# HGRN log decays in a hybrid decoder: one masked product over stacked upper and lower parts of 64 tokens, in place of two over 128

## Chip, cores and metric

The kernel runs on one core of one Trainium2 chip. The metric is the device time of one execution in microseconds. A profiled execution has in addition a span, from the first to the last instruction of the program that the profiler recorded.

## What is computed

The reference is a decoder trunk of two residual layers on 256 tokens of width 1024. Each layer has a token mixer (a group of forgetting-attention heads, "FoX", and a group of eight HGRN2 heads, merged by gates) and a channel mixer (dense SwiGLU in layer 0, eight experts with top-2 routing in layer 1). All is float32. The part that matters here is the HGRN recurrence, chunk by chunk:

```python
HG_CHUNK = 64
...
def hgrn2_recurrence(q, k, v, log_f):
    """S_t = diag(f_t) S_{t-1} + k_t v_t^T, o_t = S_t^T q_t; chunkwise. q,k,log_f: (B,S,H,dk); v: (B,S,H,dv)."""
...
    def step(state, inp):
        q_c, k_c, v_c, g_c = inp
        G = jnp.cumsum(g_c, axis=2)
        diff = G[:, :, :, None, :] - G[:, :, None, :, :]
        decay = jnp.where(causal, jnp.exp(jnp.where(causal, diff, 0.0)), 0.0)
        A = jnp.einsum('bhtk,bhsk,bhtsk->bhts', q_c, k_c, decay)
        o = jnp.einsum('bhts,bhsv->bhtv', A, v_c) + jnp.einsum('bhtk,bhkv->bhtv', q_c * jnp.exp(G), state)
```

So a pair of tokens s < t is weighted, in each of 128 key channels, by the exponential of the sum of the log decays between them.

## The kernel before

The kernel carries no state from chunk to chunk. It treats the 256 tokens as two tiles of 128 (index `i`) and writes every pair of tokens of a tile as one of seven levels (`LV` = 64, 32, ... 1): at level m, a pair lies in two neighbouring runs of m tokens. The decay from s to t is then the product of two exponentials, one from s to the border of the runs and one from the border to t. A further set, the cross decays, leads from the first tile to the second.

All the sums of log decays that these exponentials need are made by TensorE as products with masks of zeros and ones, in `hgrn` (L734). The log decays of a tile, `sg`, are split in `hgrn_in` (L699) into an upper part `lfh` in fp32r (helper `split`, L321, a cast on ScalarE) and the rest `lfl` (a subtraction on VectorE), because a product in fp32r takes its operands rounded. For each tile and head there are two PSUM banks of four masks by 128 tokens, and for each bank two products of 512 columns: L754 with `lfh`, L755 with `lfl`, summed in the bank. The contraction is over the 128 tokens of the tile. ScalarE then takes the exponential of the bank into the tile `e` (name `ee`, L756):

```python
dp = t_bank()
mf = mm.rearrange("p a t -> p (a t)")
pe.matmul(out=dp, lhsT=lfh[:, i, c0:c0 + P], rhs=mf, start=True, stop=False)
pe.matmul(out=dp, lhsT=lfl[:, i, c0:c0 + P], rhs=mf, start=False, stop=True)
a.activation(out=e[:, 4 * mi:4 * mi + 4, h, :], in_=dp.rearrange("p (a t) -> p a t", a=4), func=AF.Exp)
```

VectorE multiplies keys and queries into `e` (L766, L769; L773 to L775 for the last level), TensorE makes the small products of the levels (L785, L787, L798), VectorE gathers them in `aT` (L791 to L804), and TensorE applies them to the values (L808 to L817). There are two layers, two groups of four heads, two pairs of heads in a group and two tiles: sixteen blocks of this kind, each with two heads.

The masks are made once by GpSimd in `build_masks` (L158), during the first projections. `hgrn` is a generator: it yields between its steps, and the projection products around it (L113 to L115 from `mm3`, L411 to L413 from `turned`) advance it by `tick`, so that its steps lie between theirs. In this part of the program a scheduler settles the final order of every engine's instructions when the program is built; each engine then works its own queue in order. Weights of the projections are loaded as `raw`, cast by ScalarE (L93, `whi`) and completed by VectorE (L97, `wlo`). All PSUM tiles named `tb` share four banks, so a new log-decay product can start only when an earlier bank was read.

Of the kernel before, what the change touches and what calls it, by code (L numbers as in the profile page):

```python
# [10 lines left out]
F32 = mybir.dt.float32  # L11
F32R = mybir.dt.float32r
I32 = mybir.dt.int32
AF = mybir.ActivationFunctionType
# [3 lines left out]
P = 128  # L18
# [3 lines left out]
NT = S // P  # L22
# [18 lines left out]
def hybrid_trunk_kernel(  # L41
# [7 lines left out]
    v, a, pe, g = nc.vector, nc.scalar, nc.tensor, nc.gpsimd  # L49
# [4 lines left out]
    pre = pre_stack.enter_context(tc.tile_pool(name="pre", bufs=1, reuse_waits="tile"))  # L54
# [93 lines left out]
    ones = const.tile([P, P], F32, name="ones")  # L148
    g.memset(ones, 1.0)
    ups, iota = (const.tile([P, P], F32, name=n) for n in ("ups", "iota"))  # L150
    mAB = pre.tile([P, 9, P], F32R, tag="masks1", bufs=1, name="mAB")
    mA, mB = mAB[:, :4], mAB[:, 4:]
    mm = pre.tile([P, D], F32, tag="masks2", bufs=1, name="mm")
    cmask, up, tmask = mm[:, 0:256], mm[:, 256:384], mm[:, 384:512].bitcast(I32)
    lmask = mm[:, 512:768].bitcast(I32).rearrange("p (a t) -> p a t", a=4)
# [2 lines left out]
    def build_masks(pool):  # L158
# [7 lines left out]
        mt = u4(pool, "mt", "p (a t) -> p a t", a=8)  # L166
        g.memset(mt, 1.0)
        for li, m in enumerate(LV):
            nb = P // (2 * m)
            w = mt[:, li, :].rearrange("p (b h r) -> p b h r", b=nb, h=2)  # L170
            rt, lf = w[:, :, 1, :], w[:, :, 0, :]
            g.affine_select(out=rt, in_=rt, pattern=[[-2 * m, nb], [0, m]], compare_op=OP.is_ge, fill=0.0, base=-m, channel_multiplier=1)
            g.affine_select(out=rt, in_=rt, pattern=[[2 * m, nb], [1, m]], compare_op=OP.is_ge, fill=0.0, base=m, channel_multiplier=-1)
            g.affine_select(out=lf, in_=lf, pattern=[[-2 * m, nb], [-1, m]], compare_op=OP.is_gt, fill=0.0, base=0, channel_multiplier=1)
            g.affine_select(out=lf, in_=lf, pattern=[[2 * m, nb], [0, m]], compare_op=OP.is_gt, fill=0.0, base=m, channel_multiplier=-1)
        g.affine_select(out=mt[:, 7, :], in_=mt[:, 7, :], pattern=[[-1, P]], compare_op=OP.is_gt, fill=0.0, base=0, channel_multiplier=1)
        g.tensor_copy(mA, mt[:, 0:4])
        g.tensor_copy(mB[:, 0], mt[:, 7])
        g.tensor_copy(mB[:, 1:4], mt[:, 4:7])
        g.tensor_copy(mB[:, 4], up)  # L180
        mk = u4(pool, "mk", "p (a t) -> p a t", n=256, a=4)
        g.memset(mk, 1.0)
        for li, m in enumerate(LV[2:6]):
# [137 lines left out]
    def split(src, hi, lo):  # L321
        a.copy(hi, src)
        v.tensor_sub(lo, src, hi.bitcast(F32))
# [317 lines left out]
    def mixer(l, hT=None, first=None, half_first=None):  # L641
        with tc.tile_pool(name=f"mix{l}", bufs=1, reuse_waits="tile") as mp:
# [20 lines left out]
            if l > 0:  # L663
# [14 lines left out]
                for half in range(2):  # L678
                    tp = t_bank()
# [17 lines left out]
                return hv  # L697

            def hgrn_in(gi):  # L699
                lfh = mp.tile([P, NT, 512], F32R, tag="lfh", bufs=2, name="lfh")  # L700
                lfl = mp.tile([P, NT, 512], F32R, tag="lfl", bufs=2, name="lfl")
                kq = mp.tile([P, 2, NT, 4, P], F32, tag="kq", bufs=2, name="kq")
                c0 = O_HQ + 512 * gi
                for j, bk in enumerate(first.pop(c0) if c0 in first else proj_t(hT, win, c0, 512)):
# [2 lines left out]
                sg, kt = [], []  # L707
# [10 lines left out]
                for i in range(NT):  # L718
                    a.activation(out=sg[i], in_=sg[i], func=AF.Ln)
                for i in range(NT):  # L720
                    split(sg[i], lfh[:, i, :], lfl[:, i, :])
                for i in range(NT):
                    _, tv = transpose4(lambda b: kt[i][:, b * P:(b + 1) * P])
                    dst = kq[:, 0, i]
# [2 lines left out]
                            v.tensor_scalar(out=dst[:, b], in0=tv[:, b], scalar1=omT[:, 4 * gi + b:4 * gi + b + 1], scalar2=None, op0=OP.mult)  # L727
                    else:
                        a.copy(dst, tv)
                return lfh, lfl, kq  # L730

            aTs = []

            def hgrn(gi, lfh, lfl, kq, hv):  # L734
                if not aTs:
                    for _ in range(4):
                        aTs.append(mp.tile([P, 2, P], F32, tag="aT", bufs=4, name="aT"))
# [2 lines left out]
                for hp in range(2):  # L740
# [3 lines left out]
                    ee = []  # L744
                    for i in range(NT):
                        e = mp.tile([P, 8, 2, P], F32, tag="ee", bufs=2, name="ee")
                        ee.append(e)

                        for h in range(2):
                            c0 = (2 * hp + h) * P  # L750
                            for mi, mm in enumerate((mA, mB[:, i:i + 4])):
                                dp = t_bank()
                                mf = mm.rearrange("p a t -> p (a t)")
                                pe.matmul(out=dp, lhsT=lfh[:, i, c0:c0 + P], rhs=mf, start=True, stop=False)  # L754
                                pe.matmul(out=dp, lhsT=lfl[:, i, c0:c0 + P], rhs=mf, start=False, stop=True)  # L755
                                a.activation(out=e[:, 4 * mi:4 * mi + 4, h, :], in_=dp.rearrange("p (a t) -> p a t", a=4), func=AF.Exp)  # L756
                            yield
                        base = kq[:, 0, i, hs, :]
                        lv = [li if li < 4 or i else li + 1 for li in range(7)]
                        cross = 7 if i else 4  # L760
                        for li, m in enumerate(LV[:6]):

                            ev = e[:, lv[li]].rearrange("p h (b s r) -> p (h b) s r", s=2, r=m)
# [14 lines left out]
                        tp = t_bank()  # L778
# [14 lines left out]
                        tp = t_bank()  # L793
                        tv = tp.rearrange("p (a h r) -> p a h r", a=4, h=2)
                        for li, m in enumerate(LV[2:6]):
                            for h in range(2):
                                el = e[:, lv[2 + li], h]
                                pe.matmul(out=tv[:P - m, li, h, :].rearrange("p (b r) -> p b r", r=m), lhsT=el[:, :P - m],  # L798
                                          rhs=el.rearrange("p (b s r) -> p b s r", s=2, r=m)[:, :, 1, :], start=True, stop=True)
# [5 lines left out]
                        yield  # L805
                    tp = t_bank()
                    for h in range(2):
                        pe.matmul(out=tp[:, h * P:(h + 1) * P], lhsT=ee[0][:, 4, h], rhs=ee[1][:, 7, h], start=True, stop=True)  # L808
                    a.copy(aX, tp[:, :2 * P].rearrange("p (h t) -> p h t", h=2))
                    tp = t_bank()  # L810
                    for i in range(NT):
# [994 lines left out]
```

## Time and profile before

| | |
|---|---|
| three runs | 1912.79, 1914.8 and 1915.34 us, median 1914.8 |
| profiled execution, its own time | 1916.2 us |
| its span | 1914.5 us |
| mean granted clock of TensorE | 0.993 of 2.4 GHz |
| instructions | 25527 |
| span, forty slices | TensorE at 90% or more in all but the first two and the last |
| mixers | layer 0 up to about 400 us of the span, layer 1 from about 590 to about 900 |

Times below are counted from the start of the span. PE is TensorE with its products, PEld its weight loads, DVE VectorE, ACT ScalarE, POOL GpSimd. A product's row shows its whole passage, from first operand to last result; the next one can start while it is under way, so that the distance between two starts is shorter than the time shown for one.

### The profile page before, as it was taken

Reading aid. Unit: us, or ns where it says so; the run is one execution under the profiler, and the core shown is the slowest. Engines: PE = TensorE matmul, PEld = TensorE weight load, DVE = VectorE, ACT = ScalarE, POOL = GpSimd, SP = SyncE. Lnnn points to the kernel's source line nnn. Section 1 sums busy time; section 2 is a strip of 40 time slices with the busy share of each in tenths; the row PEclk is TensorE's granted clock in tenths of the full one; section 3 lists DMA queues with packets and bytes.
Section 4 is the critical chain, followed back from the end, with each engine's and each line's share of the span. In section 5 each row is a group of like instructions: output and inputs, shape, how many; then the busy total and the mean of one; then the engine's idle time right before and its main releaser. Section 6 shows DMA issues by size and latency. Waiting matters only on the chain.

```text
span 1914.5 us, 25527 instructions
## 1 busy us (share of the span) xinstructions
PE 1845.4 (96%) x9510; PEld 1534.2 (80%) x9510; DVE 1569.5 (82%) x2006; ACT 1309.9 (68%) x1666; POOL 210.2 (11%) x184
## 2 busy tenths in 40 slices
PE   2999999999999999999999999999999999999998
PEld 2787788889978877788787888888888888888887
DVE  6878865878858887457898989999899989999997
ACT  2467568554436765595788787787887878878775
POOL 6701200000000012100001210003100021000000
PEclk9899999999999999999999999999999999999999
DMA  9543654888855425339899999999999999999990
GB/s 301 167 156 132 220 176 142 299 302 293 314 211 172 140 88 176 120 114 338 293 347 354 349 339 370 362 376 344 340 374 359 375 346 344 368 362 369 358 364 24
DMA packets 235140, 525.50 MB, mean 274 GB/s; under 512 B 11756, under 2 KB 23292, under 8 KB 235008
## 3 DMA queue, kind: packets, MB, share of 16 engines
q1 hardware_dynamic: 233624, 523.61, 76.3%
q8 instruction: 76, 1.25, 0.3%
q14 instruction: 56, 0.46, 0.1%
q10 hardware_dynamic: 1384, 0.18, 0.1%
HBM read 522.72 MB, written 1.05 MB: 274 GB/s over the span
## 4 chain that ended last, share of the span: by engine, by line
PE 74%; DVE 2%; ACT 2%; issue 1%; POOL 1%; DVEq 0%; ACTq 0%; POOLq 0%
PE acc L114 15%; PE acc L115 15%; PE acc L113 15%; PE yb L114 5%; PE yb L115 5%; PE yb L113 5%; PE acc L412 2%; PE acc L413 2%; PE acc L411 2%; PE tb L308 2%; DVE wlo L97 1%; PE tb L1560 1%; PE tb L798 1%; POOL rs L302 1%; PE tb L1290 1%
## 5 line engine op out<-in xcount | busy, mean ns | idle before, releaser
L97 DVE TENSOR_TENSOR wlo<-raw,whi 128x1024 fp32r<-128x1024 f32 (+1 forms) x888 | 1077.1, 1237 | 141.7 <-ACT whi L93 124.5
L93 ACT CAST whi<-raw 128x1024 fp32r<-128x1024 f32 (+1 forms) x888 | 919.3, 1047 | 315.3 <-PE acc L115 183.9
L113 PE MATMUL acc<-whi,g 128*128 128x512 f32 x880 | 349.2, 397 | 0.0
L115 PE MATMUL acc<-whi,g 128*128 128x512 f32 x880 | 344.2, 391 | 0.0
L114 PE MATMUL acc<-wlo,g 128*128 128x512 f32 x880 | 344.1, 391 | 0.0
L113 PE MATMUL acc<-whi,hTh 128*128 128x512 f32 x512 | 210.2, 414 | 4.1 <-ACT hTh L615 4.1
L114 PE MATMUL acc<-wlo,hTh 128*128 128x512 f32 x512 | 206.9, 405 | 5.2 <-DVE wlo L97 5.0
L115 PE MATMUL acc<-whi,hTl 128*128 128x512 f32 x512 | 206.6, 405 | 3.5 <-DVE hTl L617 3.5
L114 PEld LDWEIGHTS acc<-wlo,g 128*128 128x128 f32 x880 | 165.5, 188 | 35.9 <-DVE wlo L97 2.8
L115 PEld LDWEIGHTS acc<-whi,g 128*128 128x128 f32 x880 | 165.1, 188 | 35.7
L113 PEld LDWEIGHTS acc<-whi,g 128*128 128x128 f32 x880 | 165.4, 188 | 32.7
L114 PE MATMUL yb<-wlo,th 128*128 128x512 f32 x440 | 172.5, 392 | 4.1 <-DVE wlo L97 4.1
L115 PE MATMUL yb<-whi,tlo 128*128 128x512 f32 x440 | 171.6, 390 | 0.0
L113 PE MATMUL yb<-whi,th 128*128 128x512 f32 x440 | 171.6, 390 | 0.0
L114 PEld LDWEIGHTS acc<-wlo,hTh 128*128 128x128 f32 x512 | 98.2, 192 | 25.4 <-DVE wlo L97 7.5
L115 PEld LDWEIGHTS acc<-whi,hTl 128*128 128x128 f32 x512 | 97.6, 191 | 24.4 <-DVE hTl L617 5.3
L411 PE MATMUL acc<-hTh,whi 128*128 128x256 f32 x416 | 117.1, 282 | 0.0
L302 POOL TENSOR_TENSOR rs<-rs,mhalf 128x8 f32<-128x8 f32 (+1 forms) x28 | 48.1, 1719 | 623.9 <-DVE rs L301 614.9
L413 PE MATMUL acc<-hTh,wlo 128*128 128x256 f32 x416 | 116.5, 281 | 0.0
L412 PE MATMUL acc<-hTl,whi 128*128 128x256 f32 x416 | 116.3, 280 | 0.0
L113 PEld LDWEIGHTS acc<-whi,hTh 128*128 128x128 f32 x512 | 97.4, 191 | 22.4 <-ACT hTh L615 5.0
L114 PEld LDWEIGHTS yb<-wlo,th 128*128 128x128 f32 x440 | 82.6, 188 | 26.0 <-DVE wlo L97 9.3
(381 smaller groups left out, 2634.8 us busy)
## 6 DMA issues: line engine op xcount, KB each, us to landing
raw<-in_moe_w_gate SPq DMA_DIRECT2D x112, 1024.0 KB, 6.3
raw<-in_moe_w_up SPq DMA_DIRECT2D x112, 1024.0 KB, 5.9
raw<-in_moe_w_down SPq DMA_DIRECT2D x110, 1024.0 KB, 5.6
raw<-in_w_in SPq DMA_DIRECT2D x66, 1024.0 KB, 5.2
raw<-in_w_ada SPq DMA_DIRECT2D x48, 1024.0 KB, 6.8
raw<-in_dense_w_gate SPq DMA_DIRECT2D x10, 1024.0 KB, 8.1
raw<-in_dense_w_up SPq DMA_DIRECT2D x10, 1024.0 KB, 7.8
raw<-in_dense_w_down SPq DMA_DIRECT2D x10, 1024.0 KB, 8.8
```

Source lines behind the costliest of these rows:

```text
L93: a.copy(hi, raw)
L97: v.tensor_sub(lo, raw, hi.bitcast(F32))
L113: pe.matmul(out=o, lhsT=lh, rhs=rh, start=start, stop=False)
L114: pe.matmul(out=o, lhsT=lh, rhs=rl, start=False, stop=False)
L115: pe.matmul(out=o, lhsT=ll, rhs=rh, start=False, stop=stop)
L302: g.tensor_tensor(out=r, in0=r, in1=mhalf[:, :shape[1]], op=OP.pow)
L308: pe.transpose(out=tp[:, b * P:(b + 1) * P], in_=src(b), identity=ident)
L411: pe.matmul(out=o, lhsT=hi, rhs=hT.hh[:, k], start=(k == 0 and c % 2 == 0), stop=False)
L412: pe.matmul(out=o, lhsT=hi, rhs=hT.hl[:, k], start=False, stop=False)
L413: pe.matmul(out=o, lhsT=lo, rhs=hT.hh[:, k], start=False, stop=(k == KD - 1 and c % 2 == 1))
L798: pe.matmul(out=tv[:P - m, li, h, :].rearrange("p (b r) -> p b r", r=m), lhsT=el[:, :P - m], rhs=el.rearrange("p (b s r) -> p b s r", s=2, ...
L1290: pe.matmul(out=tp[:, b * 2 * P:(b * 2 + ne) * P], lhsT=src[:, i, kk * P:(kk + 1) * P], rhs=pair[0]["oneh"][:, i].rearrange("p n t -> p (n ...
```

## The change

`lfh` and `lfl` become two tiles `lf[i]`, one for each token tile, with two halves `b` of 64 tokens. In half b the upper parts of its own 64 tokens lie on these tokens' partitions, and their lower parts on the other 64 partitions. One product with a mask that stands twice, once over each 64 partitions, sums both parts. A bank now holds eight masks by 64 tokens of one half. Only the cross decays need the other half's log decays; for them one product of 64 columns with a column of ones is added to one of the two banks. The mask of the level m = 64 is the one within a half, and is taken from masks that are there already.

```diff
-    mAB = pre.tile([P, 9, P], F32R, tag="masks1", bufs=1, name="mAB")
-    mA, mB = mAB[:, :4], mAB[:, 4:]
+    mAB = pre.tile([P, 2, 9, 64], F32R, tag="masks1", bufs=1, name="mAB")
...
         for li, m in enumerate(LV):
+            if not li:
+                continue
...
-        g.tensor_copy(mA, mt[:, 0:4])
-        g.tensor_copy(mB[:, 0], mt[:, 7])
-        g.tensor_copy(mB[:, 1:4], mt[:, 4:7])
-        g.tensor_copy(mB[:, 4], up)
+
+        for r in (slice(0, 64), slice(64, P)):
+            g.tensor_copy(mAB[r, 0, 2:8], mt[r, 1:7, r])
+            g.tensor_copy(mAB[r, 0, 0:2], mt[r, None, 7, r].to_broadcast([64, 2, 64]))
+            g.tensor_copy(mAB[r, 0, 8], up[r, r])
+        g.tensor_copy(mAB[:, 1], mAB[:, 0])
+        g.tensor_copy(mAB[:, 1, 1], mAB[:, 0, 8])
...
-                lfh = mp.tile([P, NT, 512], F32R, tag="lfh", bufs=2, name="lfh")
-                lfl = mp.tile([P, NT, 512], F32R, tag="lfl", bufs=2, name="lfl")
+
+                lf = [mp.tile([P, 2, 512], F32R, tag=t, bufs=2, name="lf") for t in ("lfh", "lfl")]
...
                 for i in range(NT):
-                    split(sg[i], lfh[:, i, :], lfl[:, i, :])
+                    for b, (own, other) in enumerate(((slice(0, 64), slice(64, P)), (slice(64, P), slice(0, 64)))):
+                        a.copy(lf[i][own, b], sg[i][own])
+                        v.tensor_sub(lf[i][other, b], sg[i][own], lf[i][own, b].bitcast(F32))
...
-                            for mi, mm in enumerate((mA, mB[:, i:i + 4])):
+                            for b in range(2):
                                 dp = t_bank()
-                                mf = mm.rearrange("p a t -> p (a t)")
-                                pe.matmul(out=dp, lhsT=lfh[:, i, c0:c0 + P], rhs=mf, start=True, stop=False)
-                                pe.matmul(out=dp, lhsT=lfl[:, i, c0:c0 + P], rhs=mf, start=False, stop=True)
-                                a.activation(out=e[:, 4 * mi:4 * mi + 4, h, :], in_=dp.rearrange("p (a t) -> p a t", a=4), func=AF.Exp)
+                                whole = b == i
+                                pe.matmul(out=dp, lhsT=lf[i][:, b, c0:c0 + P], rhs=mAB[:, b, i:i + 8].rearrange("p a t -> p (a t)"), start=True, stop=not whole)
+                                if whole:
+                                    pe.matmul(out=dp[:, 7 * 64 * i:7 * 64 * i + 64], lhsT=lf[i][:, 1 - b, c0:c0 + P], rhs=mAB[:, 0, 8, 63:64].to_broadcast([P, 64]), start=False, stop=True)
+                                a.activation(out=e[:, :, h, 64 * b:64 * (b + 1)], in_=dp.rearrange("p (a t) -> p a t", a=8), func=AF.Exp)
...
-                        lv = [li if li < 4 or i else li + 1 for li in range(7)]
-                        cross = 7 if i else 4
+                        lv = [li + 1 - i for li in range(7)]
+                        cross = 7 * i
...
-                        pe.matmul(out=tp[:, h * P:(h + 1) * P], lhsT=ee[0][:, 4, h], rhs=ee[1][:, 7, h], start=True, stop=True)
+                        pe.matmul(out=tp[:, h * P:(h + 1) * P], lhsT=ee[0][:, 0, h], rhs=ee[1][:, 7, h], start=True, stop=True)
```

The scheduler's order moves with this. TensorE in layer 0, at the first log-decay products, before (L411 to L413 are projection products, `tb<-mAB` are the log decays):

```order
L412 MATMUL acc<-hTl,whi 128x256
L754 MATMUL tb<-mAB,lfh 128x512 x2
L413 MATMUL acc<-hTh,wlo 128x256
L411 MATMUL acc<-hTh,whi 128x256
L755 MATMUL tb<-mAB,lfl 128x512 x2
L754 MATMUL tb<-mAB,lfh 128x512
L755 MATMUL tb<-mAB,lfl 128x512
```

And of the change, where the same lines have the numbers L415 to L417, and the log decays L760 (512 columns) and L762 (64 columns):

```order
L416 MATMUL acc<-hTl,whi 128x256
L760 MATMUL tb<-mAB,lf 128x512
L417 MATMUL acc<-hTh,wlo 128x256
L415 MATMUL acc<-hTh,whi 128x256
L416 MATMUL acc<-hTl,whi 128x256
L762 MATMUL tb<-mAB,lf 128x64
L760 MATMUL tb<-mAB,lf 128x512
```

The first log-decay product stands six projection products later than before, and three more stand between it and its bank's second product. In the whole program the order has 128 products of 512 columns on the masks before, and 64 of 512 and 32 of 64 columns in the change; casts to `lfh` and subtractions to `lfl` go from 8 and 8 on 128 partitions to 16 and 16 on 64; table loads of ScalarE go from 57 to 59.

ScalarE in layer 1, where Exp (L756) meets the Silu of the next group's queries (L705), before:

```order
L756 ACTIVATE ee<-tb 128x4x128 x2
L705 ACT_TABLE_LOAD
L705 ACTIVATE kq<-acc 128x2x256
L93 CAST whi<-raw 128x1024 x2
L705 ACTIVATE kq<-acc 128x2x256
L809 COPY aX<-tb 128x256
L756 ACT_TABLE_LOAD
L756 ACTIVATE ee<-tb 128x4x128 x4
```

And of the change (Exp is L763, Silu L709):

```order
L763 ACTIVATE ee<-tb 128x8x64
L709 ACT_TABLE_LOAD
L709 ACTIVATE kq<-acc 128x2x256
L763 ACT_TABLE_LOAD
L763 ACTIVATE ee<-tb 128x8x64
L709 ACT_TABLE_LOAD
L709 ACTIVATE kq<-acc 128x2x256
L93 CAST whi<-raw 128x1024 x2
L816 COPY aX<-tb 128x256
L763 ACT_TABLE_LOAD
L763 ACTIVATE ee<-tb 128x8x64
```

One Exp now stands between the two Silus, and the table is loaded for each of them.

## Rows read from the trace of the kernel before

**Rows 1.** Busy times on the page: us, share of the span, instructions.

```profile
PE 1845.4 (96%) x9510; PEld 1534.2 (80%) x9510; DVE 1569.5 (82%) x2006; ACT 1309.9 (68%) x1666; POOL 210.2 (11%) x184
```

**Rows 2.** Table of stretches, HGRN parts: us by engine, PEclk, DMA share, GB/s.

```profile
100.00:140.00 40.00, 39.81 (x297) 34.97 (x296) 30.42 (x69) 28.88 (x42) 0.00 (x0) 1.00 0.40 128
140.00:200.00 60.00, 58.76 (x372) 48.46 (x373) 48.36 (x119) 38.43 (x57) 7.64 (x4) 1.00 0.38 128
620.00:660.00 40.00, 39.65 (x262) 34.02 (x262) 33.47 (x65) 27.57 (x38) 0.00 (x0) 1.00 0.55 189
660.00:720.00 60.00, 56.97 (x365) 47.66 (x364) 47.10 (x119) 39.36 (x57) 5.96 (x3) 0.97 0.23 73
```

**Rows 3.** Chain of waits, 620 to 740 us: shares by line.

```profile
by line: PE acc L115 12.2%; PE acc L114 12.0%; PE acc L113 11.1%; PE tb L798 11.0%; PE tb L754 5.3%; PE tb L755 4.8%; PE tb L785 4.3%; ACT L756 3.2%; PE acc L412 3.0%; ACT ee L756 2.7%; PE acc L411 2.6%; PE acc L413 2.6%; PE tb L817 2.2%; P
```

**Rows 4.** Timeline of TensorE, layer 0: start us, us, line, operands.

```profile
133.42 0.39 PE L754 MATMUL tb<-mAB,lfh 128*128 128x512 f32 x1
...
134.11 0.39 PE L755 MATMUL tb<-mAB,lfl 128*128 128x512 f32 x1
```

**Rows 5.** Masks' tile: ns min/median/max, first and last start; idle before.

```profile
L754 PE MATMUL tb<-mAB,lfh x64: 387/396/628, 104.4 to 719.7; 128*128 128x512 f32 x64
...
L755 PE MATMUL tb<-mAB,lfl x64: 387/393/628, 105.1 to 719.9; 128*128 128x512 f32 x64
...
L180 POOL CAST mAB<-mm x1: 293/293/293, 78.4 to 78.4; 128x128 fp32r<-128x128 f32 x1
...
  ACT ee L756: 5.3, 5
```

**Rows 6.** Chain of waits, 655 to 672 us: start, us, line, count.

```profile
662.29 1.83 PE tb L798 x16
```

**Rows 7.** Timeline of TensorE: products of 256 columns, six steps.

```profile
120.71 0.28 PE L411 MATMUL acc<-hTh,whi 128*128 128x256 f32 x1
...
121.42 0.28 PE L411 MATMUL acc<-hTh,whi 128*128 128x256 f32 x1
```

**Rows 8.** Tile of the upper parts: its cast and subtraction.

```profile
L322 ACT CAST lfh<-sg x8: 606/616/622, 103.5 to 686.9; 128x512 fp32r<-128x512 f32 x8
L323 DVE TENSOR_TENSOR lfl<-sg,lfh x8: 674/687/693, 104.1 to 687.5; 128x512 fp32r<-128x512 f32 x8
```

**Rows 9.** Groups of ScalarE: busy us, mean ns, idle before.

```profile
L908 ACT ACTIVATE aqk<-tb,prm 66x512 f32<-66x512 f32 x32 | 20.2, 680 | 5.3 <-PE tb L907 5.2
```

**Rows 10.** Timeline of ScalarE, layer 1, an Exp's table load.

```profile
704.85 1.28 ACT L756 ACT_TABLE_LOAD   x1
706.15 0.60 ACT L756 ACTIVATE ee<-tb 128x512 f32<-128x512 f32 x1
```

**Rows 11.** Timeline of TensorE there; idle time in brackets.

```profile
706.80 0.54 PE L754 MATMUL tb<-mAB,lfh 128*128 128x512 f32 x1 [1.79 <-ACT ee L756]
707.14 0.63 PE L755 MATMUL tb<-mAB,lfl 128*128 128x512 f32 x1
...
710.54 0.40 PE L754 MATMUL tb<-mAB,lfh 128*128 128x512 f32 x1
```

**Rows 12.** Table of stretches, 706 to 712 us.

```profile
706.00:712.00 6.00, 5.20 (x16) 4.14 (x17) 3.99 (x11) 3.35 (x6) 2.54 (x1) 0.72 0.43 133
```

**Rows 13.** Tile of the exponentials: durations; who waited for it.

```profile
L766 DVE TENSOR_TENSOR ee<-ee,kq x96: 407/417/460, 108.5 to 724.7; 128x256 f32<-128x256 f32 x96
L756 ACT ACTIVATE ee<-tb x64: 587/598/616, 106.9 to 720.9; 128x512 f32<-128x512 f32 x64
...
L773 DVE TENSOR_TENSOR kq<-kq,ee x16: 280/284/325, 110.9 to 726.4; 128x128 f32<-128x128 f32 x16
L774 DVE RECIPROCAL ee<-ee x16: 933/944/948, 112.2 to 727.3; 128x128 f32<-128x128 f32 x16
...
  PEld tb L785: 5.2, 8
...
  PE tb L785: 2.8, 4
```

More of the change, by code (lines that the diff above doesn't have):

```diff
@@ L729, in hgrn_in, with hgrn @@
                         a.copy(dst, tv)
-                return lfh, lfl, kq
+                return lf, kq
             aTs = []
-            def hgrn(gi, lfh, lfl, kq, hv):
+            def hgrn(gi, lf, kq, hv):
                 if not aTs:
```

## The prediction

> **What bounds the kernel now.** I began with the busy times of the whole span: TensorE's matmuls are busy for 96% of it, VectorE for 82%, ScalarE for 68% [rows 1]. Such a share is an average over stages, so the next view is the table of stretches. The change touches only the HGRN blocks of the two mixers, whose first log-decay product starts at 104.4 us and whose last at 719.7 [rows 5]. In the four stretches that hold nearly all of them TensorE is busy 98.6 of 100 us (layer 0) and 96.6 of 100 (layer 1), VectorE 78.8 and 80.6, ScalarE 67.3 and 66.9, and the DMA queues are far from full [rows 2]. A busy TensorE can still be a stretched one, since its instructions overlap. So the third view is the chain of waits, from 620 to 740 us: 5.3% and 4.8% of these 120 us, 12.1 us together, are the products of L754 and L755, the very ones that the change replaces, and the other large shares are matmuls too [rows 3]. The fourth is the timeline of TensorE: products of 512 columns start every 0.23 us (0.69 us over three steps), although each is shown as 0.39 us long [rows 4]. The price of a product is this step, not its length. The program is thus bound by TensorE's issue in both stretches, with an ordered queue full of projection products that stand between the steps of the HGRN chain.
>
> **The change part by part**, on the profiled execution (1916.2 us, of which 1914.5 are the span; the three runs have a median of 1914.8, so it lies 1.4 us above them).
>
> *Products removed.* L754 and L755 issue 64 products each [rows 5]; the order of the changed kernel has 64 of 512 columns in their place. 64 fewer, at 0.23 us: **-14.7 us**.
>
> *Products added.* 32 of 64 columns, one for each pair of a head and a token tile. No row shows fp32r operands with so few columns. From above: 64-column products of plain f32 take 1.83 us for sixteen, 0.114 each [rows 6], and fp32r products of 256 columns take 0.118 (0.71 us over six steps) [rows 7]. From below: in proportion to columns, 64/512 of 0.23, an estimate of 0.029. I take 0.114, from the row with the same number of columns: **+3.6 us** (+0.9 to +3.8). The Trainium skill has a rule here ("TensorE: Matmul & The Clock Gate", section "Back-to-back issue gap"): products of 1 to 64 columns can start about 25 ns apart. By it the 32 would cost 0.8 us. The f32 row contradicts the rule for its own type, and nothing here shows it for fp32r.
>
> *The split.* Each of the 8 casts to lfh (0.616 us) and 8 subtractions to lfl (0.687 us) becomes two on half the partitions [rows 8]. A ScalarE instruction on 66 partitions and 512 elements takes 0.680 us, no less than one on 128 [rows 9], so half the partitions save nothing: ScalarE gets 8 x 0.616 = 4.9 us more, VectorE 8 x 0.687 = 5.5 us more, each spread over four places. VectorE has 19 to 21 us free in 100, ScalarE 33 [rows 2]. On the path: a complete first bank now needs both halves, so one more subtraction stands ahead of its second product, four times 0.69 = 2.8 us if nothing covers it. The order of TensorE in layer 0 shows six more 256-column products ahead of the first L754, 6 x 0.118 = 0.7 us of cover. I charge **0** (0 to 2.8). Behind the added subtractions on VectorE stand the HGRN multiplications, which wait for the Exp anyway.
>
> *Tables.* The order of ScalarE has 59 table loads instead of 57, the two more in layer 1, where Exp and Silu or Sigmoid now alternate. One load takes 1.28 us: it begins at 704.85, and the Exp behind it at 706.15 [rows 10]. What such a load costs when it meets TensorE is seen in the same place: TensorE waits 1.79 us for that Exp, and the products from 707.14 on take 3.40 us over eight steps, 0.43 each and not 0.23 [rows 11], while the granted clock of the stretch is 0.72, a part of it at 1.2 GHz and not 2.4 [rows 12]. The eight steps lose 1.6 us, so the event costs 3.4. Two new ones would cost 6.8 us, none costs nothing. I take one with a chance of a half: **+1.8 us** (0 to 6.8). The Trainium skill prices a table switch higher ("ScalarE: Activation LUTs", section "What ACT_TABLE_LOAD costs"): 1283 ns and a drain of about 1380, 2.66 us. The row agrees with the first figure alone, as the Exp starts 1.30 us after the load does, 0.02 us behind its end. By the page the two would hold ScalarE 5.3 us, by the row 2.6.
>
> *Exp and its layout.* There are 64 before and after, of 512 elements, 0.598 us each [rows 13]. They now write runs of 64 elements, not 128. I charge 0; what a slower one would do is a rival below.
>
> *Masks.* On POOL four selections go and eight copies stand where four stood. The last mask copy begins at 78.4, the first product that reads it at 104.4 [rows 5]. 25 us cover a few microseconds; without that cover the first HGRN block would wait for them.
>
> Sum: -14.7 + 3.6 + 0 + 1.8 = **-9.3 us**, 1906.9 on the profiled execution, less 1.4: **1905.5 us** as a median. Nothing behind a mixer should give this back, since dense layer and experts start when its last product is done.
>
> **The rivals.**
>
> *A. The narrow products are nearly free.* At the proportional 0.029 us the sum is -14.7 + 0.9 + 1.8 = -12.0, so **1902.8**. For it: 64 columns are an eighth of the work. Against it: both neighbouring rows take 0.11 or more a product [rows 6, 7]. The Trainium skill's rule on few columns, above, would come out within 0.1 us of this. Chance 0.22.
>
> *B. VectorE's chain sets the pace.* A block (16 of them: layers, groups, head pairs, token tiles) gains 11.1/16 = 0.69 us on TensorE, but its chain behind the Exp is untouched: seven multiplications of 0.417, two of 0.284 and a reciprocal of 0.944 us, 4.4 us [rows 13]. VectorE goes to about 81.5 and 83.3 us of a stretch now some 94 long, 0.87 to 0.89. For it: TensorE already waits 5.2 and 2.8 us for these multiplications at L785 [rows 13]. Against it: those are eight of some 190 us, and the order still has projection products to put between. If it holds in half the blocks, half of the 11.1 us goes: -5.6, and with 0.9 for the tables **1910.1**. Chance 0.18.
>
> *C. New waits eat it.* All four subtractions uncovered (2.8) and both table loads as dear as the one at 704.85 (6.8): -14.7 + 3.6 + 9.6 = -1.5, so **1913.3**. For it: the one event seen today shows that a wait is paid twice, by itself and by the clock. Against it: it is seen once today, as three of the four stretches have the full clock and the fourth 0.97 [rows 2]. Chance 0.12.
>
> *D. Slower: the Exp pays for its short runs.* Place: the 64 Exps of L756, which every HGRN block waits for. Nothing in the trace shows an activation that writes runs of 64 with a stride. If each took t longer and none of it were covered, the time would change by 64 t - 9.3, so it decides from 0.15 us on, an Exp of 0.74 us. At twice today's length (t = 0.598) half covered, it is 19.1 - 9.3 = +9.8, so **1924.6**. For it: ScalarE is in the middle of the chain, and TensorE waits for its banks at L754, 5.3 us today [rows 5]. Against it: casts and activations with runs of 512 or 128 elements all take about 0.6. Chance 0.08.
>
> That the change doesn't do what it says is excluded by the order: 128 wide products before, 64 wide and 32 narrow after.
>
> **How the numbers follow.** My forecast gets 0.40, A 0.22, B 0.18, C 0.12, D 0.08. A measurement here can tell about 0.2%, 3.8 us. Forecast and A are faster by more, and most of B (0.15 of its 0.18): faster 0.77. C and the rest of B: the same, 0.15. D: slower, 0.08. The range leaves out C and D, 0.20 in all, on the upper side: 1912.5. Below it takes in A with the event at 704.85 gone as well, -12.0 - 1.8 - 3.4 = -17.2, shortened to -15.8 as both together are unlikely: 1899.0.
>
> **What would show it right or wrong.** Right: 64 wide products 0.23 us apart and 32 narrow ones 0.11 behind which the next starts; the two HGRN stretches each some 4 to 6 us shorter; dense layer and experts as long as before; the chain's share of these products halved. The step at a narrow product decides between the forecast and A. For B, TensorE would wait longer at L785 for VectorE, with VectorE near 0.9 busy. For C, half-speed stretches would stand behind an Exp's table load, or TensorE would wait for lf. For D, the Exp's mean would be over 0.74 us. The forecast is wrong if the two stretches shorten and the end doesn't, for then something behind the mixers, which I take to follow, sets the time.

## The result, and the profile after

The changed kernel is slower. Four runs have a median of 1926.0 us (1922.83 to 1926.77) beside 1913.8 for the kernel before: a ratio of 1.0063, with a 95% interval of 1.0045 to 1.0080, so about 12 us more. The range of the prediction, 1899.0 to 1912.5, does not hold it, and the direction is wrong.

The page after, busy times (answering to [rows 1]), and the table of stretches (to [rows 2]):

```profile
PE 1843.5 (96%) x9478; PEld 1531.6 (80%) x9478; DVE 1574.7 (82%) x2014; ACT 1317.9 (69%) x1676; POOL 211.8 (11%) x184
```

```profile
100.00:140.00 40.00, 37.75 (x261) 33.19 (x260) 29.18 (x63) 28.24 (x41) 0.00 (x0) 0.91 0.37 121
140.00:200.00 60.00, 53.89 (x354) 43.76 (x353) 47.68 (x120) 38.78 (x57) 5.87 (x3) 1.00 0.30 102
620.00:660.00 40.00, 38.72 (x262) 33.24 (x262) 33.98 (x57) 30.37 (x40) 0.00 (x0) 1.00 0.62 213
660.00:720.00 60.00, 55.91 (x354) 45.92 (x355) 49.52 (x126) 43.40 (x62) 5.79 (x3) 0.94 0.22 71
```

TensorE was busy for 195.2 of these 200 us before and is for 186.3 now, its first stretch at a mean clock of 0.91 instead of 1.00 and its last at 0.94 instead of 0.97. The HGRN parts did not get shorter: TensorE has less to do in them and waits more. From the first Ln of a layer to the first FoX product it is 112.0 us before and 119.3 after in layer 0, 114.8 and 115.0 in layer 1. Everything behind a mixer is as long as it was. The profiled execution after is the fastest of the four runs, so the two traces are only 6.6 us apart in span (1914.5 and 1921.1).

The views of the tiles `lf` and `ee` (answering to [rows 5, 8, 13]; L760 are the wide log-decay products of 512 columns, L762 the narrow ones of 64, L726 and L727 the split, L763 the Exp):

```profile
L760 PE MATMUL tb<-mAB,lf x64: 388/477/793, 104.1 to 725.6; 128*128 128x512 f32 x64
...
L762 PE MATMUL tb<-mAB,lf x32: 190/192/403, 104.7 to 725.9; 128*128 128x64 f32 x32
L726 ACT CAST lf<-sg x16: 602/617/622, 102.5 to 687.6; 64x512 fp32r<-64x512 f32 x16
L727 DVE TENSOR_TENSOR lf<-sg,lf x16: 684/686/690, 103.1 to 690.1; 64x512 fp32r<-64x512 f32 x16
its engine sat idle before it (us, times) until:
  ACT ee L763: 11.3, 14
```

```profile
L763 ACT ACTIVATE ee<-tb x64: 587/597/619, 107.4 to 727.0; 128x512 f32<-128x512 f32 x64
```

The Exp takes 0.597 us as before, so rival D's mechanism is not there. Casts and subtractions of 64 partitions cost as much as those of 128, as forecast. What has grown is the waiting: TensorE stands before L760 until an Exp is done for 11.3 us in 14 places, where it was 5.3 us in 5.

The opening of the first head group shows where; a layer has two such openings, each from the Ln of a head group to the first products that need its Exps. ScalarE's timeline before, and after:

```profile
101.13 1.28 ACT L719 ACT_TABLE_LOAD   x1
...
103.48 1.12 ACT L322 CAST lfh<-sg 128x512 fp32r<-128x512 f32 x2
...
106.89 2.06 ACT L756 ACTIVATE ee<-tb 128x512 f32<-128x512 f32 x4
```

```profile
100.15 1.28 ACT L723 ACT_TABLE_LOAD   x1
101.44 1.15 ACT L723 ACTIVATE sg<-sg 128x512 f32<-128x512 f32 x2
102.50 2.53 ACT L726 CAST lf<-sg 64x512 fp32r<-64x512 f32 x4
105.06 1.07 ACT L735 COPY kq<-tb 128x512 f32<-128x512 f32 x2
106.15 1.28 ACT L763 ACT_TABLE_LOAD   x1
107.44 2.06 ACT L763 ACTIVATE ee<-tb 128x512 f32<-128x512 f32 x4
109.53 2.94 ACT L93 CAST whi<-raw 128x1024 fp32r<-128x1024 f32 x3
```

ScalarE works here without a gap, in a fixed order: Ln, casts, copies, table load, Exp, and then the casts of the next projection weights. The Exp begins 5.76 us after the Ln's table load before and 7.29 after; 1.41 of the 1.53 us are the two more casts. TensorE's timeline and the clock behind it, after:

```profile
108.18 0.28 PE L417 MATMUL acc<-hTh,wlo 128*128 128x256 f32 x1
110.63 0.38 PE L415 MATMUL acc<-hTh,whi 128*128 128x256 f32 x1 [2.17 <-DVE ee L773]
```

```profile
112.80:119.60 6.80, 6.80 (x30) 6.32 (x29) 2.62 (x7) 3.66 (x5) 0.00 (x0) 0.50 0.15 28
```

TensorE runs out of projection products, waits 2.17 us for the first multiplication behind the Exps (L773), and then has 6.8 us at half the clock, 1.2 GHz, in which it does 3.4 us less than at full. Before, it waited 0.2 us at the same place. That suggested the first theory: **theory 1**, the split costs it, through ScalarE's order. Against it stood **theory 2**, the products cost it, and later a third, that the scheduler's new order does.

### The profile page after: what moved, and what is told of

It is laid out like the page before. It is cut to its first block, busy times and chain, and to the rows that moved or that the text cites. A ratio compares the mean times of both kernels' runs of the same rounds, so it can differ in the third digit from the quotient of the medians.

```text
span 1921.1 us, 25483 instructions
## 1 busy us (share of the span) xinstructions
PE 1843.5 (96%) x9478; PEld 1531.6 (80%) x9478; DVE 1574.7 (82%) x2014; ACT 1317.9 (69%) x1676; POOL 211.8 (11%) x184
## 4 chain that ended last, share of the span: by engine, by line
PE 74%; DVE 2%; ACT 2%; POOL 1%; issue 0%; DVEq 0%; ACTq 0%; POOLq 0%
PE acc L114 15%; PE acc L115 15%; PE acc L113 15%; PE yb L114 5%; PE yb L115 5%; PE yb L113 5%; PE acc L415 2%; PE acc L417 2%; PE acc L416 2%; PE tb L312 2%; DVE wlo L97 1%; PE tb L1567 1%; POOL rs L306 1%; PE tb L805 1%; PE tb L1297 1%
## 5 line engine op out<-in xcount | busy, mean ns | idle before, releaser
L415 PE MATMUL acc<-hTh,whi 128*128 128x256 f32 x416 | 117.6, 283 | 2.2 <-DVE ee L773 2.2
L417 PE MATMUL acc<-hTh,wlo 128*128 128x256 f32 x416 | 116.9, 282 | 0.4 <-DVE wlo L97 0.4
```

What stands on the lines that cost most here:

```text
L415: pe.matmul(out=o, lhsT=hi, rhs=hT.hh[:, k], start=(k == 0 and c % 2 == 0), stop=False)
L417: pe.matmul(out=o, lhsT=lo, rhs=hT.hh[:, k], start=False, stop=(k == KD - 1 and c % 2 == 1))
```

## Experiments

**Parts alone, each with the order that the scheduler makes for it.**

```diff
# e1_split_alone (in the kernel before)
-                    split(sg[i], lfh[:, i, :], lfl[:, i, :])
+                    for r in (slice(0, 64), slice(64, P)):
+                        split(sg[i][r], lfh[r, i, :], lfl[r, i, :])
# e2_products_alone (in the changed kernel, in place of its casts and subtractions)
+                    split(sg[i], lf[i][:, 0], lf[i][:, 1])
# e3_pool_casts (in the changed kernel)
-                        a.copy(lf[i][own, b], sg[i][own])
+                        (g.tensor_copy if b else a.copy)(lf[i][own, b], sg[i][own])
# e5_no_narrow (in the changed kernel): L762 left out
```

> The kernel before with one part of the change: the split is done in halves of 64 partitions (4 casts and 4 subtractions for a head group instead of 2 and 2, each written to its old place), the products are the old ones. Theory 1 (the split costs it: the added casts stand in ScalarE's order ahead of the first Exp and of the next weights' casts, TensorE runs dry, then its clock falls): slower than before by 4 to 12 us, 1918 to 1926, with a wait of TensorE over 1 us and a stretch at half clock in layer 0 near 110 us. Theory 2 (the products cost it: the wide product behind a narrow one, the banks and the cover that TensorE's saved work gave): within 3 us of before, 1911 to 1917, no new half-clock stretch.

> The changed kernel with the old price of the split: two casts and two subtractions of 128 partitions for a head group, written to the two new tiles, so that the products read other rows than they should (the log decays of both parts are mixed, the values are not the reference's; the products, their shapes and their order stay). Theory 1: faster than before by 6 to 11 us, 1903 to 1908. Theory 2: slower than before by over 3 us still, 1917 or more.

> The changed kernel with the casts of the lower 64 tokens on POOL, which has nothing else to do there: ScalarE is back to two casts for a head group, VectorE keeps its four subtractions. Theory 1, if POOL's copies take no more than 1.6 us each: at least 6 us faster than the changed kernel, 1908 to 1920, and the first Exp of layer 0 about 1.2 us earlier behind the Ln. Theory 2: 1922 to 1929, as the changed kernel.

> The changed kernel without its 32 narrow products (left out, so that the whole-prefix level lacks the other half's sum). Theory 1: they and the dearer step of the wide product behind them cost 32 x 0.115 = 3.7 us, so 1920 to 1924. Theory 2: with them goes the dear step and the wait for banks behind it, 1904 to 1914.

Measured, as ratios to before: the split alone 1.0008 (0.9999 to 1.0017), the products alone 0.9993 (0.9984 to 1.0002), the change with POOL's casts 1.0025 (1.0015 to 1.0034), the change without its narrow products 1.0103 (1.0087 to 1.0118), 1932.85 us. Neither theory survives this as it stood: each part alone costs nothing, and less work than the change has takes 7 us more. Only the run with POOL's casts, at 1917.8 us, lies where theory 1 had it. The scheduler settles another order for each kernel (ScalarE loads a table 55 times in e1, 59 times in e2 and e3, 61 times in e5), and with it come single long waits at other places. In e3 it is this one of TensorE, in the passage to FoX:

```profile
199.27 0.80 PE L114 MATMUL acc<-wlo,hTh 128*128 128x512 f32 x1 [6.15 <-DVE wlo L97]
```

Kernels with different orders could not be compared part by part, so the order had to be held.

**The order bound.** For each layer's scheduled part, the next four kernels fix every engine's order by a table of numbers (the new instructions stand where those were that they replace, a bank's wide and narrow product where its second product stood):

```diff
+            k0 = len(nc.cur_bb.bb.instructions)
             hv = [hgrn_v(0), hgrn_v(1)]
...
+            for eng, runs in ORDERS[l].items():
...
+                for p, i in zip(row, row[1:]):
+                    tc.add_manual_dep(i, p.name, mybir.DependencyInfo(mybir.DependencyClass.NoSync, mybir.DependencyReason.DATA), reason="order")
```

> The changed kernel with TensorE, VectorE, ScalarE and GpSimd bound, in the scheduled part of both mixers, to the order that the kernel before has (each bank's products where that bank's second product stood, the two casts and the two subtractions of a token tile where its one stood). Order theory (the work got shorter, the scheduler's new order for it is worse): faster than before, 1900 to 1909. Resource theory (the added casts and the lost cover cost it in any order): 1917 or more.

> The reverse: the kernel before, its own instructions, bound to the order that the changed kernel has. Order theory: clearly slower than before, 1920 to 1940, as it carries 11 us more of products in the same bad order, with waits near 108 and 158 us again. Resource theory: within 4 us of before, 1910 to 1918.

> The changed kernel's products with the split of before (two casts and two subtractions of 128 partitions for a head group, so that the log decays of both parts are mixed and the values are not the reference's), bound to the order of before. By the sum of the prediction without its split and tables: -14.7 plus 0.9 to 3.7 for the narrow products, so 1900 to 1904 if TensorE's issue is the bound everywhere. If VectorE's chain sets the pace in half of the blocks: 1906 to 1909. If nothing of it is on the path: 1911 to 1916.

> The split in halves alone, with the products of before, bound to the order of before. Covered as the prediction has it: 0 to 2.8 us above before, 1912 to 1917. If ScalarE's added casts hold up TensorE: 4 x 1.2 us and more, 1918 or above.

| order of the kernel before | split of before | split in halves |
|---|---|---|
| products of before | 1 (1912.7 us) | p5: 1.0035 (1.0022 to 1.0048), 1919.5 |
| products of the change | p4: 1.0021 (1.0007 to 1.0035), 1915.9 | p1: 1.0054 (1.0041 to 1.0067), 1922.5 |

The new order is not needed for the loss: in the old order the change is still 0.54% slower, about what it is in its own. Nor is it harmless, as the kernel before in it (p2) is at 1.0030 (1.0018 to 1.0042), though that is less than was expected of it. So in the new order the change itself adds only some 0.3% (from 1.0030 to 1.0063, or to 1.0056 when measured again), and how its loss there divides between the work and the order is not settled. With the old order held the parts add up: 0.35% and 0.21% against 0.54%. **In that order the split costs some 7 us, and the products, 64 fewer wide ones, gain nothing.** The split alone in an order of its own, e1, cost nothing, so its price is one of this order and not of the split in any order.

Why the products gain nothing is seen in one block. TensorE before, and in p4, where the order is the same (its lines L758, L760 and L790 are the wide, the narrow and the first level products, L761 the Exp):

```profile
151.41 0.48 PE L754 MATMUL tb<-mAB,lfh 128*128 128x512 f32 x1
151.72 0.40 PE L755 MATMUL tb<-mAB,lfl 128*128 128x512 f32 x1
...
153.36 0.40 PE L115 MATMUL acc<-whi,hTl 128*128 128x512 f32 x1
...
155.68 0.45 PE L785 MATMUL tb<-ee 128*64 128x64 f32 x4 [0.99 <-DVE ee L766]
```

```profile
151.23 0.47 PE L758 MATMUL tb<-mAB,lf 128*128 128x512 f32 x1
151.55 0.19 PE L760 MATMUL tb<-mAB,lf 128*128 128x64 f32 x1
151.58 0.71 PE L758 MATMUL tb<-mAB,lf 128*128 128x512 f32 x2
152.12 0.19 PE L760 MATMUL tb<-mAB,lf 128*128 128x64 f32 x1
152.15 0.50 PE L758 MATMUL tb<-mAB,lf 128*128 128x512 f32 x1
152.49 0.40 PE L115 MATMUL acc<-whi,hTl 128*128 128x512 f32 x1
...
155.99 0.69 PE L790 MATMUL tb<-ee 128*64 128x64 f32 x12 [2.18 <-DVE ee L771]
```

The block's products take 1.26 us instead of 1.95, just the 0.69 us that the prediction reckoned. But the first product of the levels comes no earlier, and the wait ahead of it grows from 0.99 to 2.18. It waits for VectorE's first multiplication, that for the Exps, and these stand on ScalarE behind a table load, before and in p4:

```profile
152.29 1.28 ACT L756 ACT_TABLE_LOAD   x1
153.59 2.06 ACT L756 ACTIVATE ee<-tb 128x512 f32<-128x512 f32 x4
```

```profile
152.12 1.28 ACT L761 ACT_TABLE_LOAD   x1
153.41 2.06 ACT L761 ACTIVATE ee<-tb 128x512 f32<-128x512 f32 x4
```

Four Exps take 2.06 us, 0.52 a bank, while TensorE needed 0.49 a bank before and 0.32 now. What TensorE waited for such first multiplications in the whole program (us, times, longest), before and in p4, is all at the four openings:

```profile
PE tb L785 <- DVE ee L766: 2.8, 4, 1.2
```

```profile
PE tb L790 <- DVE ee L771: 6.7, 4, 2.2
```

With every TensorE instruction taken at the median step of its line and form, the two HGRN parts (from the first Ln of a layer to its first FoX product) hold some 210 us of work before and 200 in p4, 10 less; the waits in them (what a step takes beyond that median where its row carries a wait) go from 8.1 us to 14.5. In p5, with the split alone, they are 11.5, at as much half clock as before (10.2 us in the mixers). So in the traced execution of p4, the fastest of its twelve runs, the waits take back some two thirds of the gain; the rest goes to the clock, as the repeats show below.

**Is it that chain?** If ScalarE's chain at the openings takes the gain back, a shorter chain must be worth more with the new products than with the old. Both kernels in the order of before:

```diff
# q1 (in p4) and q2 (in the kernel before)
-                    a.activation(out=sg[i], in_=sg[i], func=AF.Ln)
+                    a.activation(out=sg[i], in_=sg[i], func=AF.Identity, scale=-1.0)
```

> The kernel with the new products and the old split in the order of before, with one more thing changed: Ln on ScalarE is replaced by a negation, which needs no table of its own (the decays are not the reference's). ScalarE has 49 table loads instead of 57, so the chain Ln, casts, Exp that opens each of the four head groups is 1.28 us shorter or more. If that chain, not TensorE's issue, takes back what the shorter products save: 5 to 10 us faster than the same kernel with Ln, 1906 to 1911, with the waits for the first multiplied tiles (1.3 to 2.3 us today) mostly gone. If VectorE's throughput sets the pace all along: at most 3 us faster, 1913 to 1916.

> The same replacement of Ln by a negation in the kernel before, in its own order (the decays are not the reference's). Its waits at those places are shorter (0.35 and 1.15 us in layer 0), so there is less to win: if the chain at the group starts is the reason, 0 to 4 us faster than before, 1909 to 1913. If shorter ScalarE work counts anywhere, as much as with the new products.

Ratios to before: 0.9981 (0.9971 to 0.9992) with the new products, 0.9991 (0.9981 to 1.0001) with the old. The same eight table loads less are worth 0.40% to the new products (from 1.0021), some 7.6 us, and 0.09%, 1.7 us, to the old. Both differences lie as the chain theory has them (the absolute 1912.5 and 1913.4 us are above their bands; the kernel before ran at 1914.9 beside them). But the waits did not mostly go, as was expected of the first. Those for the first multiplications fall from 6.7 to 4.4 us with the new products and from 2.8 to 1.3 with the old, and the one at the block of above is as long as it was:

```profile
154.70 0.81 PE L790 MATMUL tb<-ee 128*64 128x64 f32 x12 [2.19 <-DVE ee L771]
```

There ScalarE has to wait for TensorE's products ahead of the copy to `oh` (L823 in this kernel), and the Exp's table load stands behind that copy, whether Ln needs a table or not. A shorter chain is thus worth more to the new products, but the waits alone, 2.3 us and 1.5 shorter, do not account for 7.6 us and 1.7.

**Is it ScalarE's casts that the split costs?** The casts of the lower half on POOL, in the order of before (q4), and in a new one (q3), which the scheduler makes when the HGRN blocks advance 7 steps instead of 6 for a projection product:

> The changed kernel with the casts of the lower 64 tokens on POOL, in the order of before: ScalarE's chain as long as before, VectorE's four subtractions stay. If the two added casts on ScalarE are what the split costs in this order (6.8 us alone): 1914 to 1918, near the new products with the old split (1915.9). If VectorE's added subtractions are: 1920 to 1924, as the changed kernel in this order.

> An attempt at a better version: the changed kernel with the casts of the lower half on POOL, and 7 instead of 6 steps of the HGRN blocks for a filler product, so that the scheduler settles another order. The one with 6 lost 6.3 us in a single wait at 193 us, where VectorE held the weights' low part behind a chain of the attention block. If that wait was chance of the order: 1907 to 1913. If the saved work is lost somewhere in any order: 1914 to 1922.

The first is at 1.0012 (1.0002 to 1.0023), 1916.9 us, where the change in that order had 1.0054: with ScalarE back at two casts a group, nothing is left of the split's cost in that order, though VectorE keeps its added subtractions. The second was a miss, 1.0040 (1.0027 to 1.0053); another order was no better.

**A version with more taken off, and repeats.** POOL gets three of a group's four casts and the second tile's subtractions:

```diff
-                        a.copy(lf[i][own, b], sg[i][own])
-                        v.tensor_sub(lf[i][other, b], sg[i][own], lf[i][own, b].bitcast(F32))
+                        (g.tensor_copy if i or b else a.copy)(lf[i][own, b], sg[i][own])
+                        (g.tensor_sub if i else v.tensor_sub)(lf[i][other, b], sg[i][own], lf[i][own, b].bitcast(F32))
```

> A version of the change that takes the opening chain off the busy engines: of a head group's four casts ScalarE keeps one and POOL gets three, and of its four subtractions VectorE keeps the two of the first token tile and POOL gets the other two; the scheduler's own order. If the chain that opens a head group decides: faster than the changed kernel by 8 us or more, 1908 to 1917, and than before only if the scheduler's order leaves no single long wait. If POOL's subtractions (not measured yet) take over 2 us each, the second token tile comes late and it is 1918 or more.

> The same version in the order of before (ScalarE, VectorE, TensorE). ScalarE's chain at a group start is one cast, 0.6 us, shorter than before, so by the two runs with Ln replaced (1.28 us and more a group for 7.6 us) it should win about 0.6/1.28 of that against the new products with the old split (ratio 1.0021): 1910 to 1914, ratio 0.998 to 1.001.

> The new products with the old split in the order of before, once more, for a second profile: its twelve runs lay between 1910.7 and 1923.2, and the profile was of the fastest. If the spread is the clock, a slower run shows the same waits within 1 us each and more stretches at half clock behind them, about 3.4 us lost for each; if it is the transfers, waits for loads appear.

> The changed kernel itself once more, beside the same runs of before as the others: 1922 to 1928, ratio 1.0045 to 1.008 as in its first comparison.

Both relieved versions missed: 1.0033 (1.0017 to 1.0050) and 1.0031 (1.0017 to 1.0044). POOL's subtraction is twice VectorE's:

```profile
L726 POOL CAST lf<-sg x12: 607/612/1151, 101.8 to 689.0; 64x512 fp32r<-64x512 f32 x12
...
L727 POOL TENSOR_TENSOR lf<-sg,lf x8: 1263/1446/2159, 104.1 to 691.1; 64x512 fp32r<-64x512 f32 x8
```

but the waits at the openings that I had meant to shorten did not hang on the casts alone: the one near 154 us is 2.16 us, as in p4, since the Exp's table load still stands behind the copy to `oh`. Why f2 is as far behind q4 as it is stays open.

The second profile of p4 settles what equal runs differ by. Its span is 1915.6 us against 1909.0. The waits are the same (14.5 and 14.0 us in all, 2.18 ahead of the same product near 154), the clock is not. Two stretches of the first and of the second:

```profile
154.00:161.00 7.00, 5.01 (x47) 4.72 (x48) 5.49 (x11) 5.98 (x10) 0.00 (x0) 1.00 0.00 0
690.00:697.00 7.00, 7.00 (x42) 5.79 (x41) 6.12 (x14) 4.55 (x9) 0.00 (x0) 1.00 0.43 150
```

```profile
154.00:161.00 7.00, 7.00 (x36) 6.70 (x37) 4.64 (x9) 3.53 (x5) 0.00 (x0) 0.59 0.19 59
690.00:697.00 7.00, 7.00 (x40) 6.35 (x41) 5.81 (x12) 4.62 (x7) 0.00 (x0) 0.59 0.38 130
```

In the mixers (90 to 330 and 560 to 960 us) the first has 6.8 us at half clock, the second 27.3. Behind four waits of 1.12 to 2.18 us the second falls to half clock, and behind the same four the first does not. What decides it is not known. p4's twelve runs lie over 12.5 us, and their times follow the mean granted clock: 1923.2 us at 0.986, 1916.3 at 0.990, 1910.7 and 1911.7 at 0.994. At 0.994, the mean of the kernel before beside them (median 1912.7 us), the new products are thus 1 to 2 us ahead; it is the clock that makes a loss of it. The changed kernel's two profiles have 23.9 and 20.5 us at half clock there, the kernel before 10.2. Measured again, the changed kernel is at 1.0056 (1.0042 to 1.0069), 1924.1 us.

**A version that beats both.** ScalarE's order mended at three openings; r1 is q4 with it, r2 the kernel before with it (ScalarE loads a table 53 times in both, 57 before). It is a change of the table of numbers alone. In layer 0, at the second head group, ScalarE's order becomes:

```
before: Ln, aX, Sigmoid, Sigmoid, cast, Ln, kq, cast, kq, oh, Exp x4
now:    aX, Sigmoid, Sigmoid, Ln, Ln, cast, kq, cast, kq, Exp, oh, Exp x3
```

> An attempt to beat both: the changed kernel with the lower half's casts on POOL in the order of before (ratio 1.0012), and ScalarE's order mended by hand at three places where an Exp that TensorE waits for stands behind a table load or a copy: both Sigmoids of a head group ahead of both Lns, in layer 0 the first Exp ahead of the copy to oh, in layer 1 the attention block's Ln behind four Exps (53 table loads instead of 57). If those openings are what takes the saved work back: the waits of 2.3, 1.6 and 2.1 us at them shrink by 1.2 us or more each and the clock falls less often, 1907 to 1912, ratio 0.996 to 0.999. If not: 1914 to 1917.

> The kernel before with the same three places of ScalarE's order mended, all else in its own order. It waits less there (1.15 and 1.8 us): 1 to 4 us faster than before, ratio 0.998 to 0.9995. If the shorter products pay once the openings are mended, this one is the slower of the two; if it is the faster, the change does not pay even then.

Measured: r1 0.9984 (0.9975 to 0.9993), 1910.3 us, its eleven runs within 4.1 us; r2 0.9994 (0.9985 to 1.0004), 1912.3 us. ScalarE and TensorE of r1 at the block of above:

```profile
150.07 1.28 ACT L763 ACT_TABLE_LOAD   x1
152.79 0.60 ACT L763 ACTIVATE ee<-tb 128x512 f32<-128x512 f32 x1 [1.43 <-PE tb L762]
153.28 0.58 ACT L825 COPY oh<-tb 128x512 f32<-128x512 f32 x1
```

```profile
151.54 0.49 PE L824 MATMUL tb<-hv,aT 128*128 128x128 f32 x2 [1.65 <-DVE aT L808]
155.86 0.33 PE L792 MATMUL tb<-ee 128*64 128x64 f32 x2 [0.77 <-DVE ee L773]
```

The table is loaded while ScalarE would wait anyway, and the wait of TensorE there is 0.77 instead of 2.18. But ahead of the block it now waits 1.65 us for VectorE, where p4 had no wait above 0.5. In all, the HGRN parts of r1 hold as much waiting as those of p4 (14.6 and 14.5 us; r2 5.9), only in shorter pieces, none above 1.65 us, and its profile has 3.4 us at half clock in the mixers. Its span, 1908.9, is that of p4's fastest run, 1909.0. So what the mended order brings is mostly that the clock stays up: r1's eleven runs have mean granted clocks of 0.992 to 0.995. The change, with POOL's casts and a mended order, is then some 3 us faster than the kernel before. The intervals of r1 and r2, each taken against the kernel before, still overlap. Set against each other, r1 is 2.0 us below r2 in the median, and eight of its eleven runs are faster than r2's fastest: with both orders mended the change pays some 2 us of the 10 that TensorE has less to do.

## Why the prediction was wrong

*The bound.* The step that failed first is "The program is thus bound by TensorE's issue in both stretches". The stretches were 97 to 99% busy [rows 2], and I took that as a distance from the next bound. It was none: ScalarE's chain at the openings was already as long as TensorE's work beside it, as the waits at L754 and L785 [rows 5, 13] said. With the order held, TensorE's work shrank by 10 us, its waits grew by 6.4, and the clock behind them took the rest and more (1.0021). Rival B had the form of it, a chain of another engine behind the products, but named VectorE, where it is ScalarE's table load and Exps at the openings, and charged it with half of the gain.

*Products removed and added* (-14.7 and +3.6). The sum was right: 0.69 us a block forecast and seen. The step of a narrow product is 0.03 us, not 0.114 (151.55 to 151.58 in p4), as rival A had it; but a wide product behind a narrow or small one steps 0.31 to 0.34 (151.23 to 151.55 and 152.15 to 152.49 in p4, 151.41 to 151.72 before), not 0.23. The two together make a narrow product 0.11 to 0.14 dearer to its block, which is the forecast's 0.114 and four times rival A's price. That the row of another type came out right was luck, and the step alone, named as the sign that decides between the two, misleads. The Trainium skill ("TensorE: Matmul & The Clock Gate", section "Back-to-back issue gap") puts products of 1 to 64 columns about 25 ns apart; this trace agrees, with 0.03 us. The f32 row that I set against it [rows 6] says nothing of an fp32r step.

*The split* (0, at most 2.8). Measured with the order held: 0.35%, some 7 us (in an order of its own, 0.08%). I priced each cast right, 0.616 us, and put ScalarE's 4.9 us "spread over four places" against the 33 us that it has free in 100. Those four places are the openings, where it has none free. The bound of 2.8 counted VectorE's subtractions alone; q4 shows that in that order it was the casts.

*Tables and waits* (+1.8, at most 6.8). The event was seen rightly as a wait and half clock behind it, but it has no fixed price: the one at 110.63 cost 2.17 us and 3.4 more by the clock, 5.6 together and not 3.4, and p4's first profile has such waits with no half clock behind them. The number of events was wrong too. I counted added table loads, of which there are two; the waits come at every opening, also in p1 and p4, which have the 57 loads of before. Rival C, "new waits eat it", is what happened, but far beyond its price: it had 1913.3, measured were 1926.0.

*Exp and masks* (0 and 0). As forecast.

*The order.* I read the changed order as a fact about cover at one place (six more products ahead of L760). They were cover used up early: behind the product of 108.18 TensorE runs dry and waits 2.17 us, where the same instructions in the old order (p1) wait 1.16.

The other signs that the prediction named served: the stretches did not shorten, VectorE is busy for 76.9 and 83.5 of 100 us and not near 0.9, as rival B would have it, and half-speed stretches stand behind waits for the Exp (those from 112.8, 696.5 and 713.6 us in the first profile of the change, behind waits of 2.17, 1.38 and 1.16 us). A wait of 2.39 us at 161 has none behind it.

## What to carry to other kernels

An engine that is busy for 98% of a stretch says nothing about how near the next bound is. Before pricing a saving there, follow the chain of the other engines through one block, from its first instruction to the first product that needs its result, and compare it with the work that TensorE has in that time; the saving counts only up to the difference. Instructions that are added to the engine in the middle of such a chain can cost their whole length at each opening, however idle that engine is on average; whether they do depends on the order. A wait can be paid twice, as the clock may fall behind it: here it fell behind waits of 1.1 to 2.2 us in some runs and not in others, so that two kernels with equal waits can differ by several us. And where a scheduler makes the order, hold it before comparing parts: here the parts added up only then.

## What was not expected of the hardware

A fp32r product of 64 columns started 0.03 us ahead of the next product, but a 512-column product behind it took a step of 0.32 to 0.34 us instead of 0.23, so that the narrow product costs its block 0.11 to 0.14 us. POOL casts 64 x 512 elements in 0.61 us, as fast as ScalarE (0.62), while its subtraction of the same size takes 1.45 us against VectorE's 0.69. The Trainium skill ("GPSIMD Engine Reference", section "Engine selection") has both, one-input operations near line rate and two-input ones about twice as slow, and the trace agrees. Two executions of one kernel with equal waits had spans of 1909.0 and 1915.6 us, with 6.8 and 27.3 us at half clock in the mixers.
